# Sliding-window attention in a two-layer trunk: four heads per visit, score products alternating between the two 64-row halves of the array

## The chip, the cores and the metric

The kernel runs on one core of one Trainium2 chip. The time is the device time of one execution in microseconds (us), and the median of several runs stands for a kernel. A profile of one execution accompanies it. Engines are named as in the profile: PE is TensorE's matmul, PEld its weight load, DVE is VectorE, ACT is ScalarE, POOL is GpSimd, SP is SyncE.

## The reference

Two layers over 256 positions of width 1024. In each, one projection of the normed input feeds a gated linear recurrence and a sliding-window attention; both are merged, and a feed-forward block follows. What matters here is the attention: 16 query heads and 4 key/value heads of 64 columns, a window of 128, and one sink per query head that takes part in the softmax.

```python
def swa_with_sinks(q, k, v, sinks):
    ...
    s = jnp.einsum('bnqhgd,bnshd->bnhgqs', qb, kw).astype(jnp.float32) * (hd ** -0.5)
    ...
    mask = (delta >= 0) & (delta < WINDOW) & (kpos >= 0)
    s = jnp.where(mask[None, :, None, None], s, -jnp.inf)
    sink = sinks.astype(jnp.float32).reshape(1, 1, ATT_KV_HEADS, ATT_GROUP, 1, 1)
    m = jnp.maximum(jnp.max(s, axis=-1, keepdims=True), sink)
    p = jnp.exp(s - m)
    p = p / (jnp.sum(p, axis=-1, keepdims=True) + jnp.exp(sink - m))
    o = jnp.einsum('bnhgqs,bnshd->bnqhgd', p.astype(v.dtype), vw)
    return o.reshape(B, S, Hq * hd)
```

## The kernel before

The main stream is a sequence of projections. `proj` and `form_a` hold activations as the stationary operand and stream 512 columns of weight; `form_b` holds weights and streams 256 positions. Every f32 weight tile (`raw`, from memory) is split into two reduced-precision parts, `wh` by a cast on ACT and `wl` by a subtraction on DVE, and each product is three matmuls (`wh` with the activation's high part, `wl` with it, `wh` with its low part). Five buffers of each (`NW`) let the split run ahead of TensorE: `used()` gives a unit back and asks for the next.

All else runs beside the main stream as side work: Python generators (`keys`, `attention`, `recurrence`, the norms), which `run` advances at each `yield` of the main stream. A number that a side yields is how many main steps it sits out. A main step is six matmuls of 512 columns in the v and gate projections and twelve of 256 in the pb projection. The order in which instructions stand on each engine is then made by the tile scheduler out of this program order and its dependencies. [...]

The sixteen query heads lie in two tiles `qT[g]`, transposed, so that a head's 64 columns lie in rows 0 to 63 or 64 to 127: the row half `u` belongs to one key/value head, and `kT` holds its keys in the same half. Attention goes by pairs of heads, `kt` = 0 to 7 (`KT` = 8), two heads of one half in a visit. Round `kt` does `attend(kt)`, sits out `YA` = 2 main steps, does `turn(kt - 1)`, sits out `YB` = 2, does `values(kt - 1)`, sits out `YC` = 2:

- `attend` makes the scores. For query block t = 0 (128 keys) and t = 1 (256 keys) it issues two matmuls (tile `qk`), each with 64 contraction rows. DVE adds the mask and takes the row maximum into `stat` (the instruction is `CUSTOM_DVE_ANT_0` in the profile and `ISA` in the order), ACT takes the exponentials with their sum, DVE normalizes into `s` (tile `sp`).
- `turn` transposes the probabilities on TensorE (tile `pt`, six per visit), and ACT copies them to a second half of `sp`, `pT`.
- `values` multiplies with the values (tile `pv`): two heads, each into its own 64 output rows, that is, its own column half of the array. The result is split into `att` for the next projection.

Every PSUM tile has one 512-column bank. Tag `at` has two banks, `hg` two, and `mm` (the main stream) four. All tiles of the attention use `at` before. `spread` makes a row of scale factors by two matmuls (tile `rp`) out of two diagonal tiles `dg` that DVE writes; in the first attention rounds it stands between the v projections. The recurrence starts after the attention has ended, and shares the tag `sp` and the banks of `hg`.

Of the kernel before, what the change touches and what calls it, by code (L numbers as in the profile page):

```python
# [7 lines left out]
F32 = mybir.dt.float32  # L8
# [3 lines left out]
AF = mybir.ActivationFunctionType  # L12
ALU = mybir.AluOpType
AX = mybir.AxisListType

P = 128
D = 1024
S = 256
NT = S // P
DEPTH = 2  # L20
KT = D // P
HEADS = 8
QH = 16
KVH = 4
HD = 64
# [2 lines left out]
EPS = 1e-6  # L28
MIN_F = 1e-30
NRAW, NW = 3, 5  # L30
YA, YB, YC, YS, YO, YP, YD, YE, YQ = 2, 2, 2, 2, 2, 2, 3, 2, 5
NEG = -1e30

C_HQ, C_HF, C_HI, C_HG, C_AQ, C_AK, C_GA, C_GB = 0, 1024, 2048, 3072, 4096, 5120, 5632, 6656
# [6 lines left out]
def trunk(ctx, tc, x, norm1, w_in, lb_logits, hg_norm, attn_sinks, w_pa, w_pb, w_o, norm2,  # L41
# [18 lines left out]
    V, A, G, T = (Ordered(e) for e in (nc.vector, nc.scalar, nc.gpsimd, nc.tensor))  # L60
# [10 lines left out]
    sm = ctx.enter_context(tc.tile_pool(name="sm", bufs=2))  # L71
    pp = ctx.enter_context(tc.tile_pool(name="pp", bufs=2, space=bass.MemoryType.PSUM))

    def psum(name, tag="mm"):
        return pp.tile([P, 512], F32, tag=tag, name=name, bufs=4 if tag == "mm" else 2)

    def btile(shape, name, tag="b", dt=F32):
        return big.tile(shape, dt, tag=tag, name=name, bufs=6)

    def ztile(shape, name, tag="z", dt=F32):  # L80
        return sm.tile(shape, dt, tag=tag, name=name, bufs={"z": 4, "hx": 4, "rp": 2}[tag])
# [9 lines left out]
    ident = cp.tile([P, P], F32, tag="ident", name="ident")  # L91
# [17 lines left out]
    amask = cf[:, C_MASK:C_MASK + 256]  # L109
    nsink = cp.tile([P, DEPTH * QH], F32, tag="nsink", name="nsink")  # L110
# [148 lines left out]
    def split(hi, lo, src):  # L259
        A.copy(hi, src)  # L260
        V.tensor_tensor(lo, src, hi.bitcast(F32), ALU.subtract)
# [66 lines left out]
    def halves(name, tags="rr"):  # L328
        return [tuple(btile([P, 4, S], f"{name}{n}{g}", tags[g], F32R) for n in "hl") for g in range(2)]
# [29 lines left out]
    def layer(l, n1):  # L359
# [19 lines left out]
        def rope(buf, nh, t):  # L379
            v3 = buf.rearrange("p (h d) -> p h d", d=HD)  # L380
            co = cf[:, C_COS + 16 * t:C_COS + 16 * t + 16].rearrange("p (o c) -> p o c", o=1)
            si = cf[:, C_SIN + 16 * t:C_SIN + 16 * t + 16].rearrange("p (o c) -> p o c", o=1)
            ta = ztile([P, QH, 16], f"ropa{l}{t}{nh}", "rp")
            tb = ztile([P, QH, 16], f"ropb{l}{t}{nh}", "rp")
            V.tensor_tensor(ta[:, :nh], v3[:, :nh, 0:16], co.to_broadcast([P, nh, 16]), ALU.mult)
            V.tensor_tensor(tb[:, :nh, 0:8], v3[:, :nh, 8:16], si[:, :, 0:8].to_broadcast([P, nh, 8]), ALU.mult)
            V.tensor_tensor(tb[:, :nh, 8:16], v3[:, :nh, 0:8], si[:, :, 8:16].to_broadcast([P, nh, 8]), ALU.mult)
            V.tensor_tensor(v3[:, :nh, 0:16], ta[:, :nh], tb[:, :nh], ALU.add)

        akv = [ztile([P, 512], f"akv{l}{t}", "hx") for t in range(NT)]  # L390
        kT = ztile([P, 2, S], f"kT{l}", "hx")
        aq = [btile([P, D], f"aq{l}{t}") for t in range(NT)]
        qT = [btile([P, 4, S], f"qT{l}{g}") for g in range(2)]
# [3 lines left out]
        att = halves(f"att{l}")  # L397
# [3 lines left out]
        state = {}  # L401
# [11 lines left out]
        def queries(g):  # L413
            for t in range(NT):
                ps = psum(f"qp{l}{t}{g}", "at")
                for i in range(4):
                    T.transpose(ps[:, i * P:(i + 1) * P], aq[t][:, g * 512 + i * P:g * 512 + (i + 1) * P], ident)
                A.copy(qT[g][:, :, t * P:(t + 1) * P], ps.rearrange("p (i c) -> p i c", i=4))

        def attend(kt):  # L420
            g, u, i0 = kt // 4, (kt // 2) % 2, 2 * (kt % 2)
            pr = slice(u * 64, u * 64 + 64)
            hs = l * QH + 2 * kt
            s = state["sp"][:, kt % 2, 0]
            m = sm.tile([P, 4, 2, 2], F32, tag="stat", name=f"stat{l}{kt}", bufs=3)
            for t in range(NT):
                W = (t + 1) * P
                ps = psum(f"qk{l}{kt}{t}", "at")
                for i in range(2):
                    T.matmul(ps[:, i * W:(i + 1) * W], qT[g][pr, i0 + i, t * P:(t + 1) * P], kT[pr, g, 0:W],  # L430
                             start=True, stop=True)
                for i in range(2):
                    V.tensor_tensor_reduce(s[:, i, t * P:t * P + W], ps[:, i * W:(i + 1) * W], amask[:, 256 - W:256],
                                           op0=ALU.add, op1=ALU.max, scale=1.0, scalar=-3.0e38,
                                           accum_out=m[:, 0, t, i:i + 1])
            nsk = nsink[:, hs:hs + 2].rearrange("p (o h) -> p o h", o=1).to_broadcast([P, 2, 2])
            V.scalar_tensor_tensor(m[:, 1], m[:, 0], -0.125, nsk, ALU.mult, ALU.min)
            V.tensor_tensor(m[:, 2], m[:, 1], nsk, ALU.subtract)
            for t in range(NT):
                for i in range(2):  # L440
                    sv = s[:, i, t * P:t * P + (t + 1) * P]
                    A.activation(sv, sv, AF.Exp, bias=m[:, 1, t, i:i + 1], scale=0.125,
                                 accum_out=m[:, 0, t, i:i + 1])
            state["exp"] = A.activation(m[:, 2], m[:, 2], AF.Exp).ins
            V.tensor_tensor(m[:, 3], m[:, 0], m[:, 2], ALU.add)
            V.reciprocal(m[:, 3], m[:, 3])
            for t in range(NT):
                for i in range(2):
                    sv = s[:, i, t * P:t * P + (t + 1) * P]
                    V.tensor_scalar(sv, sv, m[:, 3, t, i:i + 1], None, ALU.mult)  # L450
            return s

        def turn(kt, s):
            pT = state["sp"][:, kt % 2, 1]
            ps = psum(f"pt0{l}{kt}", "at")
            for i in range(2):
                for t in range(NT):
                    T.transpose(ps[:, i * S + t * P:i * S + t * P + P], s[:, i, t * P:t * P + P], ident)
            A.copy(pT[:, :, 0:S], ps.rearrange("p (i c) -> p i c", i=2))
            ps = psum(f"pt1{l}{kt}", "at")  # L460
            for i in range(2):
                T.transpose(ps[:, i * P:(i + 1) * P], s[:, i, 2 * P:3 * P], ident)
            A.copy(pT[:, :, S:3 * P], ps[:, :S].rearrange("p (i c) -> p i c", i=2))
            return pT

        def values(kt, pT):
            g, kv = kt // 4, kt // 2
            po = psum(f"pv{l}{kt}", "at")
            vs = slice(256 + kv * HD, 256 + (kv + 1) * HD)
            for i in range(2):  # L470
                o = po[i * 64:i * 64 + 64, 0:S]
                T.matmul(o, akv[0][:, vs], pT[:, i, 0:S], start=True, stop=False)
                T.matmul(o[:, P:S], akv[1][:, vs], pT[:, i, S:3 * P], start=False, stop=True)
            split(att[g][0][:, kt % 4, :], att[g][1][:, kt % 4, :], po[:, :S])

        def attention():
            state["sp"] = sm.tile([P, 2, 2, 2, 384], F32, tag="sp", name=f"sp{l}", bufs=1)
            for t in range(NT):
                rope(aq[t], QH, t)
            yield YQ  # L480
            queries(0)
            yield 2
            prev = None
            for kt in range(KT + 1):
                cur = attend(kt) if kt < KT else None
                yield YA
                if prev is not None:
                    pT = turn(kt - 1, prev)
                    yield YB
                    values(kt - 1, pT)  # L490
                if kt == 1:
                    queries(1)
                prev = cur
                yield YC

        def decays(g):
# [203 lines left out]
        if l == 0:  # L700
            tables()
        finish(ksd)
        atd = start(attention(), 1)
        for c in range(2):
            if c == 1:
                spread()
            yield from proj(f"v{c}", lambda t, ps: evac_scaled(v[t][:, c * 512:(c + 1) * 512], ps, rs[t]))
        for g in range(2):
            for dst in fqk[g][:2]:
                for b in range(2):  # L710
                    ps = psum(f"pb{l}{g}{b}").rearrange("p (a c) -> p a c", a=2)
# [221 lines left out]
    for l in range(DEPTH):  # L933
        hold = []

        def whole():
            hold.append((yield from layer(l, nx)))

        run(whole())
        nx = hold[0]  # L940
# [53 lines left out]
```

## Time and profile before

| | before |
|---|---|
| median of 3 runs (lowest to highest) | 973.53 us (973.47 to 973.94) |
| the profiled execution, its own time | 973.66 us |
| its span, first to last instruction | 971.8 us |
| mean granted TensorE clock | 0.997 |
| instructions | 16199 |
| matmul records on PE | 6666 |
| attention, layer 0, first to last score product | starts at 57.8 us |
| attention, layer 1, last score product | 616.7 us |

In the profile an f32 matmul is two records on PE and two weight loads on PEld. A row of the timeline gives the start, the length, the engine, the line (all are line 55, a helper that issues everything), the operation, out<-in, the shape and how many records were merged; in brackets is idle time ahead and what ended it. Main matmuls overlap, so that the step from start to start is what one costs, not its length.

### The profile page before, as it was taken

The page shows a single profiled execution, that of the slowest core. Times are in us where ns is not written, and L with a number is a line of the kernel's source. Part 1 is how long each engine was busy: PE and PEld are TensorE (multiplying, and loading weights), DVE is VectorE, ACT ScalarE, POOL GpSimd, SP SyncE. Part 2 cuts the span into 40 slices and gives each one's busy share as a digit, 9 for nine tenths or more (in the row PEclk, how much of TensorE's full clock was granted, in tenths as well). Part 3 has the DMA queues.
Part 4 walks back from the last instruction along what each step waited for, and adds up shares of the span by engine and source line. Part 5 has one row for each costly group of instructions (what it writes and reads, how often), then busy time and mean ns, then how long its engine had stood idle before and what let it go on. Part 6 is the DMA issues. An engine that isn't in the chain of part 4 may idle for free.

```text
span 971.8 us, 16199 instructions
## 1 busy us (share of the span) xinstructions
PE 956.2 (98%) x6666; PEld 837.7 (86%) x6666; DVE 642.3 (66%) x1072; ACT 503.2 (52%) x810; POOL 17.8 (2%) x28
## 2 busy tenths in 40 slices
PE   7999999999999999999999999999999999999996
PEld 5879987788889999999878899887788899999995
DVE  6566667987587656555475666689857766556554
ACT  6556559555545444444365655775454544444442
POOL 1000000010000000000000000000000000000000
PEclk9999999999999999999999999999999999999998
DMA  8644444554445555655465444445545465555641
GB/s 281 228 153 131 131 131 131 174 172 133 171 150 185 188 177 192 195 175 189 157 209 182 130 131 133 130 132 173 172 152 174 153 195 193 197 173 182 203 136 44
DMA packets 110938, 161.24 MB, mean 166 GB/s; under 512 B 2769, under 2 KB 64401, under 8 KB 110865
## 3 DMA queue, kind: packets, MB, share of 16 engines
q1 hardware_dynamic: 110160, 159.12, 50.6%
q8 instruction: 52, 0.85, 0.3%
q10 hardware_dynamic: 704, 1.10, 0.3%
q14 instruction: 22, 0.17, 0.1%
HBM read 159.15 MB, written 1.05 MB: 165 GB/s over the span
## 4 chain that ended last, share of the span: by engine, by line
PE 91%; DVE 5%; ACT 2%; issue 1%; DMA 0%; POOL 0%; POOLq 0%; ACTq 0%; SPq 0%
PE pg L55 13%; PE pu L55 13%; PE acc L55 12%; PE pb L55 10%; PE ga L55 5%; PE v L55 5%; PE wo L55 5%; PE ya L55 5%; PE aq L55 4%; PE yb L55 3%; PE gate L55 3%; PE qk L55 3%; PE akv L55 2%; PE gb L55 2%; DVE wl L55 1%
## 5 line engine op out<-in xcount | busy, mean ns | idle before, releaser
L55 ACT CAST wh<-raw 128x1024 fp32r<-128x1024 f32 x300 | 314.4, 1049 | 358.9 <-PE pg L55 71.6
L55 DVE TENSOR_TENSOR wl<-raw,wh 128x1024 fp32r<-128x1024 f32 x300 | 366.5, 1223 | 199.3 <-ACT wh L55 198.0
L55 PE MATMUL pg<-xh_n,wh 128*128 128x256 f32 x352 | 99.8, 284 | 0.0
L55 PE MATMUL pu<-xh_n,wh 128*128 128x256 f32 x352 | 99.8, 283 | 0.0
L55 PE MATMUL pg<-xl_n,wh 128*128 128x256 f32 x352 | 99.7, 284 | 0.0
L55 PE MATMUL pu<-xh_n,wl 128*128 128x256 f32 x352 | 99.6, 283 | 0.0
L55 PE MATMUL pu<-xl_n,wh 128*128 128x256 f32 x352 | 99.6, 283 | 0.0
L55 PE MATMUL pg<-xh_n,wl 128*128 128x256 f32 x352 | 99.6, 283 | 0.0
L55 PE MATMUL pb<-xh_n,wh 128*128 128x256 f32 x256 | 75.4, 294 | 0.0
L55 PE MATMUL pb<-xl_n,wh 128*128 128x256 f32 x256 | 72.4, 283 | 0.0
L55 PE MATMUL pb<-xh_n,wl 128*128 128x256 f32 x256 | 72.4, 283 | 0.0
L55 PE MATMUL acc<-wl,ah 128*128 128x512 f32 x176 | 68.8, 391 | 0.0
L55 PE MATMUL acc<-wh,al 128*128 128x512 f32 x176 | 68.5, 389 | 0.0
L55 PE MATMUL acc<-wh,ah 128*128 128x512 f32 x176 | 68.3, 392 | 0.0
L55 PEld LDWEIGHTS pg<-xl_n,wh 128*128 128x128 f32 x352 | 67.5, 192 | 0.4
L55 PEld LDWEIGHTS pg<-xh_n,wh 128*128 128x128 f32 x352 | 67.5, 192 | 0.4
L55 PEld LDWEIGHTS pu<-xh_n,wh 128*128 128x128 f32 x352 | 67.6, 192 | 0.0
L55 PEld LDWEIGHTS pu<-xl_n,wh 128*128 128x128 f32 x352 | 67.6, 192 | 0.0
L55 PEld LDWEIGHTS pu<-xh_n,wl 128*128 128x128 f32 x352 | 67.6, 192 | 0.0
L55 PEld LDWEIGHTS pg<-xh_n,wl 128*128 128x128 f32 x352 | 67.5, 192 | 0.0
L55 PEld LDWEIGHTS pb<-xh_n,wh 128*128 128x128 f32 x256 | 48.9, 191 | 5.0 <-issue 5.0
L55 PEld LDWEIGHTS pb<-xl_n,wh 128*128 128x128 f32 x256 | 48.9, 191 | 0.0
(232 smaller groups left out, 1886.3 us busy)
## 6 DMA issues: line engine op xcount, KB each, us to landing
raw<-in_w_in SPq DMA_DIRECT2D x58, 1024.0 KB, 5.1
raw<-in_w_gate SPq DMA_DIRECT2D x22, 1024.0 KB, 5.2
raw<-in_w_up SPq DMA_DIRECT2D x22, 1024.0 KB, 5.2
raw<-in_w_down SPq DMA_DIRECT2D x22, 1024.0 KB, 5.0
raw<-in_w_pb SPq DMA_DIRECT2D x8, 1024.0 KB, 5.0
raw<-in_w_pa SPq DMA_DIRECT2D x8, 1024.0 KB, 5.1
raw<-in_w_o SPq DMA_DIRECT2D x8, 1024.0 KB, 5.0
raw<-in_w_in SPq DMA_DIRECT2D x4, 512.0 KB, 7.0
```

The source lines that it names most:

```text
L55: ins = call(*args, **kw)
```

## The change

Attention goes in four groups `n` of four heads, two heads in each row half, instead of eight pairs. `attend(n)` issues eight score matmuls; within a query block they alternate between the halves `u` = 0 and 1, which write to different PSUM banks. Block t = 0 uses the two `at` banks, t = 1 the two `hg` banks. The vector work per visit is twice as much (eight reduces, eight exponentials, eight normalizations), the statistics are computed per query block, and the number of heads in all is unchanged. `turn(n)` makes twelve transposes into three banks and copies back over `s` itself (three copies for four heads instead of four). `values(n)` does the products of four heads in one visit, for one key/value head after the other, with two banks. The main steps between become `YA`, `YB`, `YC` = 4, 3, 4; five rounds take the place of nine.

```diff
-YA, YB, YC, YS, YO, YP, YD, YE, YQ = 2, 2, 2, 2, 2, 2, 3, 2, 5
+YA, YB, YC, YS, YO, YP, YD, YE, YQ = 4, 3, 4, 2, 2, 2, 3, 2, 5
...
-        def attend(kt):
-            g, u, i0 = kt // 4, (kt // 2) % 2, 2 * (kt % 2)
-            pr = slice(u * 64, u * 64 + 64)
-            s = state["sp"][:, kt % 2, 0]
+        def attend(n):
+            g, i0 = n // 2, 2 * (n % 2)
+            s = state["sp"][:, n % 2]
...
-                ps = psum(f"qk{l}{kt}{t}", "at")
+                pss = [psum(f"qk{l}{n}{t}{u}", "hg" if t else "at") for u in range(2)]
                 for i in range(2):
-                    T.matmul(ps[:, i * W:(i + 1) * W], qT[g][pr, i0 + i, t * P:(t + 1) * P], kT[pr, g, 0:W],
-                             start=True, stop=True)
+                    for u in range(2):
+                        pr = slice(u * 64, u * 64 + 64)
+                        T.matmul(pss[u][:, i * W:(i + 1) * W], qT[g][pr, i0 + i, t * P:(t + 1) * P], kT[pr, g, 0:W],
+                                 start=True, stop=True)
...
-        def turn(kt, s):
-            pT = state["sp"][:, kt % 2, 1]
-            ps = psum(f"pt0{l}{kt}", "at")
-            for i in range(2):
+        def turn(n):
+            s = state["sp"][:, n % 2]
+            for u in range(2):
+                ps = psum(f"pt{l}{n}{u}", "at")
                 for i in range(2):
...
+                A.copy(s[:, 2 * u:2 * u + 2, 0:S], ps.rearrange("p (i c) -> p i c", i=2))
+            ps = psum(f"pt{l}{n}2", "hg")
+            for i in range(4):
                 T.transpose(ps[:, i * P:(i + 1) * P], s[:, i, 2 * P:3 * P], ident)
+            A.copy(s[:, :, S:3 * P], ps.rearrange("p (i c) -> p i c", i=4))
...
+        def values(n):
+            g, pT = n // 2, state["sp"][:, n % 2]
+            pos = [psum(f"pv{l}{n}{u}", "at") for u in range(2)]
+            for u in range(2):
+                vs = slice(256 + (2 * g + u) * HD, 256 + (2 * g + u + 1) * HD)
+                for i in range(2):
+                    o = pos[u][i * 64:i * 64 + 64, 0:S]
+                    T.matmul(o, akv[0][:, vs], pT[:, 2 * u + i, 0:S], start=True, stop=False)
+                    T.matmul(o[:, P:S], akv[1][:, vs], pT[:, 2 * u + i, S:3 * P], start=False, stop=True)
...
-            for kt in range(KT + 1):
-                cur = attend(kt) if kt < KT else None
+            for n in range(5):
+                if n < 4:
+                    attend(n)
                 yield YA
-                if prev is not None:
-                    pT = turn(kt - 1, prev)
+                if n:
+                    turn(n - 1)
                     yield YB
-                    values(kt - 1, pT)
-                if kt == 1:
+                    values(n - 1)
+                if n == 1:
                     queries(1)
```

Where the instructions stand now is shown at three places of layer 0. The first is PE at the first score products, between two matmuls of the v projection (`v_0` and `v_1` are its two PSUM tiles); before:

```order
L55 MATMUL v_1_480<-wl_454,xh_n_0_109 128x512
L55 MATMUL v_1_480<-wh_453,xl_n_0_110 128x512
L55 MATMUL qk_575<-kT_165,qT_168 128x128 x2
L55 MATMUL qk_580<-kT_165,qT_168 128x256 x2
L55 MATMUL v_0_608<-wh_506,xh_n_0_109 128x512
```

And now:

```order
L55 MATMUL v_1_480<-wh_453,xl_n_0_110 128x512
L55 MATMUL qk_575<-kT_165,qT_168 128x128
L55 MATMUL qk_576<-kT_165,qT_168 128x128
L55 MATMUL qk_575<-kT_165,qT_168 128x128
L55 MATMUL qk_576<-kT_165,qT_168 128x128
L55 MATMUL qk_585<-kT_165,qT_168 128x256
L55 MATMUL qk_586<-kT_165,qT_168 128x256
L55 MATMUL qk_585<-kT_165,qT_168 128x256
L55 MATMUL qk_586<-kT_165,qT_168 128x256
L55 MATMUL v_0_628<-wh_506,xh_n_0_109 128x512
```

Four matmuls in one half became eight that alternate between a tile of half 0 (575, 585) and one of half 1 (576, 586); in all other visits they stand the same way, but for the second of layer 1, where the halves change in blocks of one to three matmuls.

The second place is PE at the two `rp` matmuls of `spread`, a few main steps later; before, 26 main matmuls stand between the first score products and the first of them:

```order
L55 MATMUL v_0_608<-wl_541,xh_n_0_109 128x512
L55 MATMUL rp_n_0_600<-dg_n_00_601,ones 128x128
L55 MATMUL qk_645<-kT_165,qT_168 128x128 x2
L55 MATMUL v_0_608<-wh_540,xl_n_0_110 128x512
L55 MATMUL v_1_609<-wh_540,xh_n_0_109 128x512
L55 MATMUL rp_n_0_600<-dg_n_01_604,ones 128x128
L55 MATMUL v_1_609<-wl_541,xh_n_0_109 128x512
L55 MATMUL v_1_609<-wh_540,xl_n_0_110 128x512
L55 MATMUL qk_650<-kT_165,qT_168 128x256 x2
```

And now, behind 37 main matmuls (in layer 1 behind 43):

```order
L55 MATMUL v_0_628<-wh_570,xh_n_0_109 128x512
L55 MATMUL rp_n_0_620<-dg_n_00_621,ones 128x128
L55 MATMUL v_0_628<-wl_571,xh_n_0_109 128x512
L55 MATMUL v_0_628<-wh_570,xl_n_0_110 128x512
L55 MATMUL v_1_629<-wh_570,xh_n_0_109 128x512
L55 MATMUL v_1_629<-wl_571,xh_n_0_109 128x512
L55 MATMUL v_1_629<-wh_570,xl_n_0_110 128x512
L55 MATMUL rp_n_0_620<-dg_n_01_624,ones 128x128
```

The second visit, which the `rp` matmuls cut in two before, now follows them whole.

The third place is DVE from the reduces of the first visit to the diagonal tiles `dg` that `rp` reads; before:

```order
L55 ISA sp_487,stat_574<-qk_580,cf 128x256
L55 ISA stat_574 128x1
L55 TENSOR_TENSOR wl_623<-raw_522,wh_622 128x1024
L55 SCALAR_TENSOR_TENSOR stat_574<-stat_574,nsink 128x4
L55 TENSOR_TENSOR stat_574<-stat_574,nsink 128x4
L55 TENSOR_TENSOR stat_574<-stat_574 128x4
L55 RECIPROCAL stat_574<-stat_574 128x4
L55 TENSOR_SCALAR sp_487<-sp_487,stat_574 128x128 x2
L55 TENSOR_SCALAR sp_487<-sp_487,stat_574 128x256 x2
L55 TENSOR_SCALAR dg_n_00_601<-ident,r_n_00_113 128x128
L55 TENSOR_TENSOR wl_641<-raw_522,wh_640 128x1024
L55 TENSOR_SCALAR dg_n_01_604<-ident,r_n_01_114 128x128
```

And now, where the four 128-column reduces stand ahead of a `wl` and the four 256-column ones behind it:

```order
L55 ISA sp_487,stat_574<-qk_586,cf 128x256
L55 ISA stat_574 128x1
L55 SCALAR_TENSOR_TENSOR stat_574<-stat_574,nsink 128x4 x2
L55 TENSOR_TENSOR stat_574<-stat_574,nsink 128x4 x2
L55 TENSOR_TENSOR stat_574<-stat_574 128x8
L55 RECIPROCAL stat_574<-stat_574 128x8
L55 TENSOR_SCALAR sp_487<-sp_487,stat_574 128x128 x4
L55 TENSOR_SCALAR sp_487<-sp_487,stat_574 128x256 x4
L55 TENSOR_SCALAR dg_n_00_621<-ident,r_n_00_113 128x128
L55 TENSOR_TENSOR wl_661<-raw_522,wh_660 128x1024
L55 TENSOR_SCALAR dg_n_01_624<-ident,r_n_01_114 128x128
```

The diagonal tiles and the next `wl` moved behind twice the vector work of a visit.

More of the change, by code (lines that the diff above doesn't have):

```diff
@@ L418, in queries @@
                 A.copy(qT[g][:, :, t * P:(t + 1) * P], ps.rearrange("p (i c) -> p i c", i=4))
-        def attend(kt):
-            g, u, i0 = kt // 4, (kt // 2) % 2, 2 * (kt % 2)
-            pr = slice(u * 64, u * 64 + 64)
-            hs = l * QH + 2 * kt
-            s = state["sp"][:, kt % 2, 0]
-            m = sm.tile([P, 4, 2, 2], F32, tag="stat", name=f"stat{l}{kt}", bufs=3)
+        def attend(n):
+            g, i0 = n // 2, 2 * (n % 2)
+            s = state["sp"][:, n % 2]
+            m = sm.tile([P, 4, 2, 2, 2], F32, tag="stat", name=f"stat{l}{n}", bufs=3)
@@ L432, in attend @@
                 for i in range(2):
[L433 to L437, printed above, removed]
@@ L438, in attend @@
-            V.tensor_tensor(m[:, 2], m[:, 1], nsk, ALU.subtract)
-            for t in range(NT):
-                for i in range(2):
-                    sv = s[:, i, t * P:t * P + (t + 1) * P]
-                    A.activation(sv, sv, AF.Exp, bias=m[:, 1, t, i:i + 1], scale=0.125,
-                                 accum_out=m[:, 0, t, i:i + 1])
+                    for u in range(2):
+                        V.tensor_tensor_reduce(s[:, 2 * u + i, t * P:t * P + W], pss[u][:, i * W:(i + 1) * W],
+                                               amask[:, 256 - W:256], op0=ALU.add, op1=ALU.max, scale=1.0,
+                                               scalar=-3.0e38, accum_out=m[:, 0, t, u, i:i + 1])
@@ new lines, in attend @@
+            nsk = nsink.rearrange("p (l g u h) -> p l g u h", l=DEPTH, g=2, u=2)[:, l, g, :, i0:i0 + 2]
+            for t in range(NT):
+                V.scalar_tensor_tensor(m[:, 1, t], m[:, 0, t], -0.125, nsk, ALU.mult, ALU.min)
+                V.tensor_tensor(m[:, 2, t], m[:, 1, t], nsk, ALU.subtract)
+            for t in range(NT):
+                for u in range(2):
+                    for i in range(2):
+                        sv = s[:, 2 * u + i, t * P:t * P + (t + 1) * P]
+                        A.activation(sv, sv, AF.Exp, bias=m[:, 1, t, u, i:i + 1], scale=0.125,
+                                     accum_out=m[:, 0, t, u, i:i + 1])
@@ L447, in attend @@
             for t in range(NT):
-                for i in range(2):
-                    sv = s[:, i, t * P:t * P + (t + 1) * P]
-                    V.tensor_scalar(sv, sv, m[:, 3, t, i:i + 1], None, ALU.mult)
-            return s
-        def turn(kt, s):
-            pT = state["sp"][:, kt % 2, 1]
-            ps = psum(f"pt0{l}{kt}", "at")
[L456 to L461, printed above, removed]
-                T.transpose(ps[:, i * P:(i + 1) * P], s[:, i, 2 * P:3 * P], ident)
-            A.copy(pT[:, :, S:3 * P], ps[:, :S].rearrange("p (i c) -> p i c", i=2))
-            return pT
@@ L466, in values @@
[L466 to L474, printed above, removed]
+                for u in range(2):
+                    for i in range(2):
+                        sv = s[:, 2 * u + i, t * P:t * P + (t + 1) * P]
+                        V.tensor_scalar(sv, sv, m[:, 3, t, u, i:i + 1], None, ALU.mult)
@@ new lines, in turn @@
+        def turn(n):
+            s = state["sp"][:, n % 2]
+            for u in range(2):
+                ps = psum(f"pt{l}{n}{u}", "at")
+                for i in range(2):
+                    for t in range(NT):
+                        T.transpose(ps[:, i * S + t * P:i * S + t * P + P], s[:, 2 * u + i, t * P:t * P + P], ident)
+                A.copy(s[:, 2 * u:2 * u + 2, 0:S], ps.rearrange("p (i c) -> p i c", i=2))
+            ps = psum(f"pt{l}{n}2", "hg")
+            for i in range(4):
+                T.transpose(ps[:, i * P:(i + 1) * P], s[:, i, 2 * P:3 * P], ident)
+            A.copy(s[:, :, S:3 * P], ps.rearrange("p (i c) -> p i c", i=4))
@@ new lines, in values @@
+        def values(n):
+            g, pT = n // 2, state["sp"][:, n % 2]
+            pos = [psum(f"pv{l}{n}{u}", "at") for u in range(2)]
+            for u in range(2):
+                vs = slice(256 + (2 * g + u) * HD, 256 + (2 * g + u + 1) * HD)
+                for i in range(2):
+                    o = pos[u][i * 64:i * 64 + 64, 0:S]
+                    T.matmul(o, akv[0][:, vs], pT[:, 2 * u + i, 0:S], start=True, stop=False)
+                    T.matmul(o[:, P:S], akv[1][:, vs], pT[:, 2 * u + i, S:3 * P], start=False, stop=True)
+            for u in range(2):
+                kk = 2 * u + n % 2
+                split(att[g][0][:, kk, :], att[g][1][:, kk, :], pos[u][:, :S])
@@ L476, in attention @@
         def attention():
-            state["sp"] = sm.tile([P, 2, 2, 2, 384], F32, tag="sp", name=f"sp{l}", bufs=1)
+            state["sp"] = sm.tile([P, 2, 4, 384], F32, tag="sp", name=f"sp{l}", bufs=1)
             for t in range(NT):
@@ L482, in attention @@
             yield 2
-            prev = None
-            for kt in range(KT + 1):
-                cur = attend(kt) if kt < KT else None
+            for n in range(5):
+                if n < 4:
+                    attend(n)
                 yield YA
-                if prev is not None:
-                    pT = turn(kt - 1, prev)
+                if n:
+                    turn(n - 1)
                     yield YB
-                    values(kt - 1, pT)
-                if kt == 1:
+                    values(n - 1)
+                if n == 1:
                     queries(1)
-                prev = cur
                 yield YC
```

## The prediction

> **What bounds the kernel now.** I read the page's engine shares first, then the chain that ended last, then the waits.
>
> ```profile
> PE 956.2 (98%) x6666; PEld 837.7 (86%) x6666; DVE 642.3 (66%) x1072; ACT 503.2 (52%) x810; POOL 17.8 (2%) x28
> PEclk9999999999999999999999999999999999999998
> PE 91%; DVE 5%; ACT 2%; issue 1%; DMA 0%; POOL 0%; POOLq 0%; ACTq 0%; SPq 0%
> ACT wh L55 <- PE pg L55: 71.6, 44, 2.3
> ```
>
> TensorE is busy 98% of the span at a full granted clock and carries 91% of the chain. The casts that prepare weights wait for TensorE (ACT waits for PE to give a weight buffer back), not the other way round. So whatever takes time on TensorE comes off the end, one for one, as long as nothing new makes TensorE wait. All the rest is an account of TensorE time. I price a visit (a run of small matmuls between two matmuls of the main projection) by the start of the second main matmul behind it minus the start of the last one ahead of it, minus two ordinary steps.
>
> **A visit of score products (qk).** From the timeline of PE and the view of the tile qk:
>
> ```profile
> 57.25 0.39 PE L55 MATMUL v<-wl,xh_n 128*128 128x512 f32 x1
> 57.48 0.39 PE L55 MATMUL v<-wh,xl_n 128*128 128x512 f32 x1
> 57.80 1.57 PE L55 MATMUL qk<-kT,qT 64*128 64x128 f32 x8
> ...
> 59.64 0.40 PE L55 MATMUL v<-wl,xh_n 128*128 128x512 f32 x1
> ...
> 615.53 1.50 PE qk L55 x8
> L55 PE MATMUL qk<-kT,qT x128: 272/374/480, 57.8 to 616.7; 64*128 64x128 f32 x64, 64*128 64x256 f32 x64
> ```
>
> The main step is 57.48 - 57.25 = 0.23. The visit costs 59.64 - 57.48 - 0.46 = 1.70. It holds eight passes (each f32 matmul is two), four with 128 and four with 256 columns, all in one 64-row half. The 128 passes of the trace are 16 visits of eight, one for each of 8 head pairs in 2 layers; the piece of the chain at 615.53 is the last visit's. How much of 1.70 is streaming and how much is entering and leaving the 64-row form? One visit of layer 0 was cut in two by the scheduler, with rp matmuls around it:
>
> ```profile
> 65.10 0.39 PE L55 MATMUL v<-wl,xh_n 128*128 128x512 f32 x1
> 65.33 0.38 PE L55 MATMUL rp_n<-dg_n,ones 128*128 128x128 f32 x2
> 65.64 0.71 PE L55 MATMUL qk<-kT,qT 64*128 64x128 f32 x4
> ...
> 66.61 0.40 PE L55 MATMUL v<-wh,xh_n 128*128 128x512 f32 x1
> 66.84 0.38 PE L55 MATMUL rp_n<-dg_n,ones 128*128 128x128 f32 x2
> ...
> 67.30 0.40 PE L55 MATMUL v<-wh,xl_n 128*128 128x512 f32 x1
> 67.62 1.13 PE L55 MATMUL qk<-kT,qT 64*128 64x256 f32 x4
> ...
> 69.02 0.39 PE L55 MATMUL v<-wl,xh_n 128*128 128x512 f32 x1
> ```
>
> 66.61 - 65.10 - 0.46 = 1.05 for rp and the 128 part; 67.30 - 66.61 - 0.46 = 0.23 for an rp alone; 69.02 - 67.30 - 0.46 = 1.26 for the 256 part. So the cut visit costs 1.05 - 0.23 + 1.26 = 2.08 where a whole one costs 1.70. The same eight passes with one more entry and exit: a switch costs 0.38, streaming 1.32. Before, qk takes 14 x 1.70 + 2 x 2.08 = 28.0 us (the second visit of layer 1 is cut in the same way, and I take the same price).
>
> **Do two halves run side by side?** No row of before mixes the two row halves in one visit, so this is the unknown. The nearest row is the product with the values (pv), which writes two column halves:
>
> ```profile
> 86.23 0.28 PE L55 MATMUL pb<-xl_n,wh 128*128 128x256 f32 x1
> 86.35 0.28 PE L55 MATMUL pb<-xh_n,wl 128*128 128x256 f32 x1
> 86.56 0.88 PE L55 MATMUL pv<-sp,akv 128*64 128x256 f32 x8
> ...
> 87.59 0.28 PE L55 MATMUL pb<-xl_n,wh 128*128 128x256 f32 x1
> L55 PE MATMUL pv<-sp,akv x128: 272/326/431, 73.7 to 633.9; 128*64 128x256 f32 x64, 128*64 128x128 f32 x64
> 73.70 0.20 PEld L55 LDWEIGHTS pv<-sp,akv 128*64 128x64 f32 x4 [0.35 <-ACT wh L55]
> 78.46 0.41 PEld L55 LDWEIGHTS qk<-kT,qT 64*128 64x128 f32 x3
> ```
>
> A pv visit has the same eight passes, four of 256 and four of 128 columns, and costs 87.59 - 86.35 - 0.24 = 1.00. With the same switch of 0.38 that is 0.62 of streaming, 0.47 of the 1.32 in a qk visit. Two column halves therefore run side by side here, and their weight loads too: four loads lie within 0.20, while three qk loads in one half take 0.41, 0.11 apart. Ends for the new qk visit, which has sixteen passes: side by side 1.32 + 0.38 = 1.70 (the pv row), one after the other 2.64 + 0.38 = 3.02 (the qk row). I take 1.70: the two halves have their own rows of the array and, in the new code, their own PSUM banks, so they are apart in the same sense as the two column halves are.
>
> **The sum, part by part.**
> - qk: 16 visits become 8. At 1.70 each 13.6 instead of 28.0: -14.4 (at 3.02 each: -3.8).
> - pv: 16 visits of 1.00 become 8 with twice the streaming and one switch, 1.24 + 0.38 = 1.62: 13.0 instead of 16.0, -3.0. Ends: 0, if the switch stood inside the streaming, and -3.0.
> - Transposes (pt): equal in number, 12 per visit instead of 6. Their rows show no switch to save:
>
> ```profile
> 82.83 0.28 PE L55 MATMUL pb<-xh_n,wl 128*128 128x256 f32 x1
> 82.95 0.82 PE L55 MATMUL pt<-ident,sp 128*128 128x128 f32 x6
> ...
> 83.72 0.28 PE L55 MATMUL pb<-xl_n,wh 128*128 128x256 f32 x1
> ```
>
> 83.72 - 82.83 - 0.24 = 0.65 for six, 0.11 each, which is their streaming: 0. One copy from PSUM less per four heads falls on ACT, which is 52% busy: 0.
> - The in-place turned probabilities (s is overwritten) add a wait: the reduces of visit n+2 write where the pv matmuls of visit n read. In the order two visits lie between, so it is over: 0.
> - Twelve main steps per four heads (2 x 6) become 11, and five rounds of 11 replace nine of 6: the attention ends one step later (62 against 61), and the recurrence after it starts one step later, in the same visits: 0. The sigmoids that follow the last exp move ahead, under projections: 0.
> - The vector work of a visit doubles and lies in one stretch. Who waits for it? In layer 0 the rp matmul, behind a dg on DVE that stands behind the whole chain of the first visit:
>
> ```profile
> 58.54 0.29 DVE L55 CUSTOM_DVE_ANT_0 sp<-qk,cf 128x128 f32<-128x128 f32 x1 [1.90 <-PE qk L55]
> 58.76 0.29 DVE L55 CUSTOM_DVE_ANT_0 sp<-qk,cf 128x128 f32<-128x128 f32 x1
> 59.41 0.43 DVE L55 CUSTOM_DVE_ANT_0 sp<-qk,cf 128x256 f32<-128x256 f32 x1 [0.35 <-PE qk L55]
> 60.10 1.22 DVE L55 TENSOR_TENSOR wl<-raw,wh 128x1024 fp32r<-128x1024 f32 x1
> 61.24 0.15 DVE L55 SCALAR_TENSOR_TENSOR stat<-stat,nsink 128x4 f32<-128x4 f32 x1
> 61.43 0.40 ACT L55 ACTIVATE sp<-sp,stat 128x128 f32<-128x128 f32 x1 [1.91 <-DVE stat L55]
> 63.42 0.16 DVE L55 TENSOR_TENSOR stat<-stat 128x4 f32<-128x4 f32 x1 [1.83 <-ACT stat L55]
> 63.84 1.01 DVE L55 TENSOR_SCALAR sp<-sp,stat 128x128 f32<-128x128 f32 x4
> 64.76 0.28 DVE L55 TENSOR_SCALAR dg_n<-ident,r_n 128x128 f32<-128x128 f32 x1
> ```
>
> In the new order four reduces of 0.22 (58.54 to 58.76) start at 58.54, then wl (60.10 to 61.24: 1.14), four of 0.35 (59.41 to 60.10 is two), one step of statistics 0.19: the exps begin at 62.1. They took 61.43 to 63.42 = 1.99, with about 0.2 of it the last small one; twice as many take 3.8: 65.9. Then 0.42 and twice 0.92 (63.84 to 64.76): dg starts at 68.2 and is usable at 68.6. The rp stands behind 37 main matmuls instead of 26; the second of them starts at 59.64, so TensorE is there at 59.64 + 36 x 0.23 = 67.9. It waits 0.7 us. In layer 1 the rp stands behind 43, 1.4 us more, and does not wait: +0.7 in all (ends: 0 and 2). The weights themselves have more room: the next wl is written by 70, and TensorE needs it after a unit of 24 pb matmuls that follows the second visit, some 6 us later.
>
> [...]
>
> Sum: -14.4 - 3.0 + 0.7 = -16.7. The profiled execution took 973.66 with a span of 971.8; the median of the runs is 973.53, 0.1 away. 973.53 - 16.7 = **956.8 us**.
>
> **Rivals.**
> 1. The halves overlap only in part (960.1). For it: no row shows loads into two row halves. If the sixteen loads still come 0.11 apart, they bound the visit: 16 x 0.11 + 0.38 = 2.14, eight of them 17.1, so -10.9 - 3.0 + 0.5 = -13.4. Against it: the pv loads lie together. [...]
> 2. The change does not do what it says: the halves run one after the other. Then qk gives -3.8 and pv -3.0, rp comes late enough for its dg: 966.7. Against it: pv.
> 3. Slower: a change of the row half costs like a change of form. A visit then has seven changes, eight visits 56. The switch of 0.38 is an entry and an exit, 0.19 each; 56 x 0.19 = 10.6 on top of serial visits gives -6.8 + 10.6 = +3.8: 977.3. It decides against the change from 6.8 / 56 = 0.12 us per change. For it: entering a form does cost. Against it: in pv the column half changes within the visit and 0.62 leaves no room for it.
>
> **Chances.** Side by side 0.72 (956.8; its own range is 954.8 to 960: streams that shrink to 0.47 as in pv, 8 x (1.24 + 0.38) = 13.0, and no wait give 973.53 - 15.0 - 3.0 = 955.5, less the spread of the runs; no saving at pv gives 959.8). Rival 1 0.10, rival 2 0.08, rival 3 0.10, in which a price near 0.12 leaves 0.03 within no change. The range 954.8 to 963.0 holds the first two cases, 0.82, less a little for waits I did not see. 0.2% is 1.9 us, about what this kernel's runs can tell from no change; faster by more: 0.72 + 0.10 + 0.08 = 0.90; the same 0.03; slower 0.07.
>
> **What would show it.** In the trace after: eight qk visits of sixteen passes, each with a cost near 1.70 (2.1: rival 1; 3.0: rival 2; above 3.0: rival 3); pv visits near 1.62; DVE busy unchanged, with about 0.7 us of TensorE idle ahead of the first rp of layer 0 and none in layer 1; the span near 955.1. A new wait of PE for wl or wh within the attention would make the forecast too low; so would a wait of the qp matmuls for the PSUM banks that both pv now hold.

## The result, and the profile after

The changed kernel takes 957.56 us (957.36 to 957.66) against 973.68 us for the kernel before on the same chip (973.47 to 973.94): a ratio of 0.9834, 95% interval 0.9817 to 0.9851. The change is worth 16.1 us; 16.7 was forecast (956.8). The profiled execution has a span of 955.8, 16.0 less than before.

From the page of the changed kernel: busy time of the engines, granted TensorE clock by slices, the shares of the chain that ended last.

```profile
span 955.8 us, 16173 instructions
PE 940.6 (98%) x6666; PEld 830.2 (87%) x6666; DVE 639.3 (67%) x1056; ACT 502.6 (53%) x794; POOL 16.4 (2%) x28
PEclk9999999999999999999999999999999999999999
PE 96%; ACT 1%; DMA 1%; DVE 1%; issue 0%; POOL 0%; POOLq 0%; ACTq 0%
```

The number of matmul records is the same (6666), the mean granted clock is 0.998 (0.997 before), and TensorE is still busy 98% of the span. Its busy time fell by 15.6 (956.2 to 940.6), so nearly all of the gain is TensorE time; little of it is idle time of TensorE that went away.

The timeline of PE at the first score visit of the changed kernel (start, length, shape, records merged):

```profile
57.30 0.39 PE L55 MATMUL v<-wh,xl_n 128*128 128x512 f32 x1
57.62 1.58 PE L55 MATMUL qk<-kT,qT 64*128 64x128 f32 x16
59.13 0.50 PE L55 MATMUL v<-wh,xh_n 128*128 128x512 f32 x1
59.46 0.40 PE L55 MATMUL v<-wl,xh_n 128*128 128x512 f32 x1
```

59.46 - 57.30 - 0.46 = 1.70: sixteen passes cost what eight cost before. Seven of the eight score visits cost 1.70 or 1.71. The eighth is the second of layer 1. The timeline of PE there:

```profile
539.50 0.39 PE L55 MATMUL v<-wh,xl_n 128*128 128x512 f32 x1
539.73 0.38 PE L55 MATMUL rp_n<-dg_n,ones 128*128 128x128 f32 x2
540.04 2.46 PE L55 MATMUL qk<-kT,qT 64*128 64x128 f32 x16
...
542.65 0.28 PE L55 MATMUL pb<-xl_n,wh 128*128 128x256 f32 x1
```

The groups of PE by shape from 540.0 to 540.9, then the timeline of ACT:

```profile
L55 PE MATMUL qk<-kT,qT 64*128 64x128 f32 x4 | 0.7, 297 | 0.0
L55 PE MATMUL qk<-kT,qT 64*128 64x256 f32 x2 | 0.6, 378 | 0.0
```

```profile
539.23 1.38 ACT L55 ACTIVATE v<-v,r_n 128x512 f32<-128x512 f32 x2 [1.17 <-PE v L55]
540.51 0.36 ACT L55 COPY rb_n<-rp_n 128x256 f32<-128x256 f32 x1
```

The two steps around it are 0.23 and 0.12, so rp and qk cost 542.65 - 539.50 - 0.35 = 2.80 together, and 2.58 without the 0.22 of an rp. The rp tile holds one of the two `at` banks until ACT has copied it, and ACT gets to that at 540.51, behind the scaling of v. The 128-column products of half 1 need that bank, and it is free at 540.87 (540.51 + 0.36). Until 540.9 only six of the sixteen passes have started, all of half 0. The other ten are the products that need the bank and those that stand behind them in the order of this visit.

The timeline of PE at the first rp of layer 0, the row of PE's waits that belongs to it, and the first dg on DVE's timeline:

```profile
67.42 0.39 PE L55 MATMUL v<-wh,xh_n 128*128 128x512 f32 x1
68.46 0.49 PE L55 MATMUL rp_n<-dg_n,ones 128*128 128x128 f32 x2 [0.65 <-DVE dg_n L55]
...
69.02 0.40 PE L55 MATMUL v<-wh,xl_n 128*128 128x512 f32 x1
```

```profile
PE rp_n L55 <- DVE dg_n L55: 0.7, 1, 0.7
```

```profile
68.12 0.28 DVE L55 TENSOR_SCALAR dg_n<-ident,r_n 128x128 f32<-128x128 f32 x1
```

The rp waits 0.65 for its diagonal tile and costs 69.02 - 67.42 - 0.46 = 1.14 instead of 0.23. Layer 1 has no such wait. Last, the timeline of PE at the first visit with the values:

```profile
84.53 0.28 PE L55 MATMUL pb<-xh_n,wl 128*128 128x256 f32 x1
84.74 1.57 PE L55 MATMUL pv<-sp,akv 128*64 128x256 f32 x16
...
86.46 0.28 PE L55 MATMUL pb<-xl_n,wh 128*128 128x256 f32 x1
```

86.46 - 84.53 - 0.24 = 1.69, the same for all eight.

### The profile page after: what moved, and what is told of

It reads as the page before. It is cut to its first block, busy times and chain, and to the rows that moved or that the text cites. A ratio compares the mean times of both kernels' runs of the same rounds, so it can differ in the third digit from the quotient of the medians.

```text
span 955.8 us, 16173 instructions
## 1 busy us (share of the span) xinstructions
PE 940.6 (98%) x6666; PEld 830.2 (87%) x6666; DVE 639.3 (67%) x1056; ACT 502.6 (53%) x794; POOL 16.4 (2%) x28
## 3 DMA queue, kind: packets, MB, share of 16 engines
HBM read 159.15 MB, written 1.05 MB: 168 GB/s over the span
## 4 chain that ended last, share of the span: by engine, by line
PE 96%; ACT 1%; DMA 1%; DVE 1%; issue 0%; POOL 0%; POOLq 0%; ACTq 0%
PE pg L55 13%; PE pu L55 13%; PE acc L55 12%; PE pb L55 10%; PE yb L55 5%; PE ga L55 5%; PE gb L55 5%; PE gate L55 5%; PE ya L55 5%; PE wo L55 5%; PE aq L55 5%; PE v L55 4%; PE akv L55 2%; PE qk L55 1%; PE pv L55 1%; PE o L55 1%
```

## The experiments

The theory: the two row halves stream side by side, a visit pays its switch once, and every microsecond of TensorE comes off the end. The rivals: the gain comes from the longer visits alone; it depends on the strict alternation of the halves; what is saved at the rp matmuls comes back elsewhere. All kernels but the two repeats of the changed kernel have `spread` one projection earlier, called the early spread here, so that neither wait of the rp matmuls disturbs the score visits.

**The early spread itself.**

```diff
-            if c == 1:
+            if c == 0:
                 spread()
```

> One edit: spread (the dg tiles on DVE and the rp matmuls) is called ahead of the first v projection instead of ahead of the second. Theory: the wait of rp for dg in layer 0 goes (rp cost 1.14 there, 0.23 elsewhere: 0.9 us), and the second visit of layer 1, whose order was broken because a bank was still held by rp, becomes a whole one (2.58 there against 1.70: 0.9 us): 957.56 - 1.8 = 955.8. Rival (these are hidden, or the dg and rp wait elsewhere): no change, 957.6.

Measured: 957.46 us (956.89 to 957.79), ratio 0.9829 [0.9815, 0.9844], no change against the changed kernel. All eight score visits cost 1.70 now, 13.6 together, and no wait for dg is left in PE's list of waits. But the rp matmuls did not get cheap. The timeline of PE in layer 0:

```profile
52.52 0.39 PE L55 MATMUL v<-wl,xh_n 128*128 128x512 f32 x1
52.93 0.49 PE L55 MATMUL rp_n<-dg_n,ones 128*128 128x128 f32 x2
...
53.48 0.40 PE L55 MATMUL v<-wh,xh_n 128*128 128x512 f32 x1
```

This rp costs 53.48 - 52.52 - 0.46 = 0.50, since its dg stands behind a wl on DVE (the wl takes 1.22 from 51.38, the dg starts at 52.59, the rp at 52.93), and the second one 0.48, where 0.23 is what an rp costs without a wait. A visit of the query transposes (qp) then waits for the bank of a pv tile and costs 0.77 instead of 0.44. In the trace layer 0 gives about 0.1 and layer 1 about 0.7; of the 1.8 that the two waits are worth, 0.8 shows. The profiled execution also reached its 120th projection matmul 1.1 later than that of the changed kernel, all of it in the first 40 us, and that hid the rest. The early spread is not the reason of the late start: the two kernels with cut visits below have it too and reach that matmul only 0.2 and 0.3 later, the two repeats of the changed kernel 0.4 to 0.5 later. The kernels that follow were forecast from 955.8; what counts is their distance from the 957.46 measured here.

**One half for all.** Do two halves run side by side? This kernel leaves the second half of the rows out: its heads get scores from the first half's queries and keys.

```diff
-                        pr = slice(u * 64, u * 64 + 64)
+                        pr = slice(0, 64)
```

> All score products use row half 0 (the products of the second half are made from the first half's queries and keys, so those heads hold other scores); spread is called one projection earlier, as in e4_early_spread, so that rp is out of the way. Counts, shapes, banks and order are those of e4. Theory (the gain is the overlap of the two row halves): nothing can overlap, a qk visit of sixteen passes costs 2 x 1.32 + 0.38 = 3.02 instead of 1.70, eight of them 10.6 us more than e4: about 966.4. Rival (the gain is in fewer, longer visits and their place): visits stay near 1.70 and the time near e4's 955.8.

Measured: 967.52 us, ratio 0.9932 [0.9915, 0.9948], 10.1 above the early spread. The timeline of PE at the first score visit:

```profile
59.26 0.39 PE L55 MATMUL v<-wh,xl_n 128*128 128x512 f32 x1
59.58 2.88 PE L55 MATMUL qk<-kT,qT 64*128 64x128 f32 x16
...
62.74 0.40 PE L55 MATMUL v<-wl,xh_n 128*128 128x512 f32 x1
```

The same sixteen passes in the same order, all in one half, cost 62.74 - 59.26 - 0.46 = 3.02, the serial end of the forecast (3.02) to the last digit. Eight visits take 24.1 instead of 13.6, 10.5 more; the time is 10.1 more, and the qp visit no longer costs its extra 0.33 here. The banks, the counts and the order are the same, so the overlap of the halves is shown, and it alone is worth 10 us.

**Blocks of two and of four matmuls.** Must the halves alternate matmul by matmul? In the first kernel a half does two matmuls (four passes) before the other does two:

```diff
-                for i in range(2):
-                    for u in range(2):
+                for u in range(2):
+                    for i in range(2):
                         pr = slice(u * 64, u * 64 + 64)
```

> On top of e4: within a query block both matmuls of half 0 come first, then both of half 1 (blocks of four passes instead of two). Theory (each half is fed as a stream of its own, as the column halves of pv are, where blocks of four passes overlap fully): a visit stays at 1.70, the time at e4's 955.8. Rival (strict order, only neighbours across a change of half overlap): three changes per visit instead of seven, the visit near 2.5, eight of them 6 to 7 us more: about 962.

In the second all four matmuls (eight passes) of one half stand before those of the other, and the order is pinned:

```diff
+            every = [[psum(f"qk{l}{n}{t}{u}", "hg" if t else "at") for u in range(2)] for t in range(NT)]
+            for u in range(2):
+                for t in range(NT):
...
+                    for i in range(2):
...
+                        T.matmul(every[t][u][:, i * W:(i + 1) * W], qT[g][pr, i0 + i, t * P:(t + 1) * P],
+                                 kT[pr, g, 0:W], start=True, stop=True)
...
```

> On top of e4: all four matmuls of half 0 first (both query blocks, eight passes), then the four of half 1. Theory (two streams without a limit on how far ahead one may run): 1.70 per visit, 955.8. Rival, a limited look ahead, for which the broken visit of layer 1 speaks, where half 1 began only behind six passes of half 0: the visit lies between 1.70 and 3.02, and if nothing overlaps, at 3.02 and 966.4. I lean to the rival, near 2.6 and 963.

Measured: blocks of two 957.64 us, ratio 0.9832 [0.9817, 0.9847]; blocks of four 961.40, ratio 0.9870 [0.9856, 0.9885], which is 3.9 above the early spread. The timelines of PE at the first visit, first of blocks of two, then of blocks of four:

```profile
59.00 0.39 PE L55 MATMUL v<-wh,xl_n 128*128 128x512 f32 x1
59.32 1.68 PE L55 MATMUL qk<-kT,qT 64*128 64x128 f32 x16
...
61.27 0.39 PE L55 MATMUL v<-wl,xh_n 128*128 128x512 f32 x1
```

```profile
59.17 0.39 PE L55 MATMUL v<-wh,xl_n 128*128 128x512 f32 x1
59.49 2.13 PE L55 MATMUL qk<-kT,qT 64*128 64x128 f32 x16
...
61.89 0.39 PE L55 MATMUL v<-wl,xh_n 128*128 128x512 f32 x1
```

61.27 - 59.00 - 0.46 = 1.81 and 61.89 - 59.17 - 0.46 = 2.26, between 1.70 and 3.02. Where does the second half begin in the last case? Its groups of PE by shape, first in 59.48 to 60.03 and then in 60.31 to 60.47 (a group holds what runs in that stretch):

```profile
L55 PE MATMUL qk<-kT,qT 64*128 64x128 f32 x4 | 0.7, 297 | 0.0
...
L55 PE MATMUL qk<-kT,qT 64*128 64x128 f32 x3 | 0.6, 306 | 0.0
L55 PE MATMUL qk<-kT,qT 64*128 64x256 f32 x2 | 0.6, 377 | 0.0
```

and the changed kernel in the first 0.55 us of its visit:

```profile
L55 PE MATMUL qk<-kT,qT 64*128 64x128 f32 x8 | 0.7, 298 | 0.0
```

In 0.55 us the changed kernel starts eight 128-column passes, four of each half; blocks of four start only four, those of the first half. In the later stretch these have ended (they started before 60.03; the first takes 0.37, the others 0.27), and yet three 128-column passes run beside two of 256 columns. The three are of the second half, while two of the first half's four 256-column passes, which stand ahead of them in the program, have not started. The visit is 2.26 - 1.70 = 0.56 longer, which is the time of the four passes that ran alone. A bank that comes free late is not the reason: the second visit, at 72.66, has the same 2.13 from its first pass to its end as the one above, and the early spread uses the same banks at the same places and has visits of 1.70. So the change of half need not stand at every matmul: four passes of one half ahead of the other cost 0.11 a visit, eight cost 0.56; what sets these two costs no run shows. The rival of a strict order (2.5 a visit in blocks of two) falls with the 1.81, and the theory of two streams without a limit (1.70 in blocks of four) with the 2.26, which lies in the range of its rival (1.70 to 3.02) and below the 2.6 that I leaned to. The theory of 1.70 in blocks of two misses by the 0.11, which the time does not tell from the early spread (957.64 against 957.46).

**Visits cut in two.** Is the length of a visit worth anything? One kernel puts a main step of projection between the two query blocks of a score visit, the other between the two key/value heads of a visit with the values; the step is taken from the pause that follows.

```diff
+                if t:
+                    yield 1
                 W = (t + 1) * P
```

> The kernel with the early spread, and each score visit cut in two by one main step of projection between its 128-column part and its 256-column part; nothing else moves. Theory (a visit pays 0.38 once for leaving and entering the full form, and the rest is streaming): eight more switches, 8 x 0.38 = +3.0 on 957.5: 960.5, each of the sixteen half visits 0.38 plus 0.44 or 0.88. Rival (the gain is the overlap of the two halves alone, a longer visit brings nothing): 957.5.

```diff
             for u in range(2):
+                if u:
+                    yield 1
                 vs = slice(256 + (2 * g + u) * HD, 256 + (2 * g + u + 1) * HD)
```

> The kernel with the early spread, and each visit of products with the values cut in two between its two key/value heads, as in the kernel before; nothing else moves. Theory (switch of 0.38 once per visit): half visits of 1.00 as before, 2 x 1.00 - 1.69 = 0.31 more for each of eight, +2.5 to +3.0 on 957.5: 960.0 to 960.5. Rival (the switch lies inside the streaming): 957.5.

Measured: 960.12 us, ratio 0.9858 [0.9844, 0.9872], and 959.67, ratio 0.9853 [0.9839, 0.9867]: 2.7 and 2.2 above the early spread. The timeline of PE with the score visits cut, then with the value visits cut (one half visit of the second group):

```profile
58.53 0.39 PE L55 MATMUL v<-wh,xl_n 128*128 128x512 f32 x1
58.85 0.72 PE L55 MATMUL qk<-kT,qT 64*128 64x128 f32 x8
...
59.84 0.39 PE L55 MATMUL v<-wl,xh_n 128*128 128x512 f32 x1
...
60.76 0.40 PE L55 MATMUL v<-wh,xl_n 128*128 128x512 f32 x1
61.09 1.13 PE L55 MATMUL qk<-kT,qT 64*128 64x256 f32 x8
...
62.49 0.40 PE L55 MATMUL v<-wl,xh_n 128*128 128x512 f32 x1
```

```profile
106.24 0.28 PE L55 MATMUL pb<-xh_n,wl 128*128 128x256 f32 x1
106.45 0.88 PE L55 MATMUL pv<-sp,akv 128*64 128x256 f32 x8
...
107.48 0.28 PE L55 MATMUL pb<-xl_n,wh 128*128 128x256 f32 x1
```

The halves of a score visit cost 59.84 - 58.53 - 0.46 = 0.85 and 62.49 - 60.76 - 0.46 = 1.27, together 0.41 more than the 1.71 of the whole one. A half visit with the values costs 107.48 - 106.24 - 0.24 = 1.00, twice that is 0.31 more than 1.69. The times are a little under eight times these (3.3 and 2.5), in the first kernel because the qp visit got its 0.33 back. So a switch costs 0.4 at the scores and 0.3 at the values, and the length of the visits is worth its part.

**Both rp waits taken away.** The dg tiles get two buffers and are written before the aq projection; the rp matmuls stand ahead of the first v projection. The changed kernel ran beside it unchanged.

```diff
+        def diag(self):
+            self.dg = [sm.tile([P, P], F32, tag="dg", name=f"dg_{self.name}{t}", bufs=2) for t in range(NT)]
+            for t in range(NT):
+                tc.keep_in_program_order(V.tensor_scalar(self.dg[t], ident, self.r[t], None, ALU.mult))
...
         ksd = start(keys(), 1)
+        n1.diag()
...
-            if c == 1:
+            if c == 0:
                 spread()
```

> The changed kernel as it is, timed beside the three that follow. Every theory: 957.6, and again a first rp of layer 0 that waits about 0.65 for its dg, and a second score visit of layer 1 that costs about 2.6 where the others cost 1.70.

> Takes both waits away that the rp matmuls brought to the changed kernel: both dg tiles have buffers of their own and are written before the aq projection, and the rp matmuls stand ahead of the first v projection in both layers. Theory (TensorE time alone counts, and the waits were worth their TensorE time): in layer 0 the two rp cost 0.3 instead of 1.37, one qp visit may still cost 0.33 more for its bank; in layer 1 the rp cost 0.3 instead of 0.45 and the second score visit 1.70 instead of 2.58. Together -1.07 + 0.33 - 0.15 - 0.88 = -1.8: 955.8. Rival (as in the kernel with the early spread, the time comes back elsewhere, whatever is done with rp): 957.5, no change.

Measured: 957.48 us (957.25 to 957.68), ratio 0.9831 [0.9817, 0.9845]; the changed kernel beside it 957.84 (957.62 to 958.00), ratio 0.9833 [0.9820, 0.9847]. By the time alone the rival holds. The repeat of the changed kernel shows both losses again: a wait of 0.6 for dg, and 2.80 for the rp and the second score visit of layer 1. The trace says where: PE's waits and its timeline in layer 0's second norm:

```profile
PE rp_n L55 <- DVE dg_n L55: 0.6, 2, 0.3
```

```profile
294.47 0.45 PE L55 MATMUL rp_n<-dg_n,ones 128*128 128x128 f32 x2
295.19 0.49 PE L55 MATMUL rp_n<-dg_n,ones 128*128 128x128 f32 x2 [0.27 <-DVE dg_n L55]
```

In the two attentions together this kernel gains 1.6 on the changed kernel beside it. But the second norm uses `spread` too, and there the two rp matmuls now come one behind the other instead of some 3.8 us apart, each behind its dg: 1.05 and 1.11 for the two norms, where 0.5 was paid. My edit brought 1.1 back; the next kernel leaves the second norm as it was.

```diff
             for t in range(NT):
-                dg = sm.tile([P, P], F32, tag="dg", name=f"dg_{self.name}{t}", bufs=1)
-                tc.keep_in_program_order(V.tensor_scalar(dg, ident, self.r[t], None, ALU.mult))
+                if self.dg is None:
+                    dg = sm.tile([P, P], F32, tag="dg2", name=f"dg_{self.name}{t}", bufs=1)
+                    tc.keep_in_program_order(V.tensor_scalar(dg, ident, self.r[t], None, ALU.mult))
+                else:
+                    dg = self.dg[t]
                 T.matmul(rp[:, t * P:(t + 1) * P], ones, dg, start=True, stop=True)
...
```

> As the kernel with the early diagonal, but the second norm of each layer keeps one buffer and the order that it has in the changed kernel, with its two rp matmuls apart. Theory: that norm's rp cost 1.05 and 1.11 in the kernel with the early diagonal, 0.49 a layer with the matmuls apart, so 1.2 comes back and the 1.6 gained in the two attentions stays: 957.5 - 1.2 = 956.3, and 1.5 under the changed kernel run beside it. Rival (what is saved there returns elsewhere whatever is done): no change against the changed kernel, within 0.4.

> The changed kernel as it is, beside the other. Every theory: 957.6 to 957.9.

Measured: 956.28 us (956.02 to 956.46), ratio 0.9819 [0.9805, 0.9832]; the changed kernel beside it 957.98 (957.78 to 958.15), ratio 0.9836 [0.9823, 0.9850]. The runs of the two do not touch, and the difference is 1.7. The timeline of PE in layer 0, where the four passes of both rp now stand in one visit without a wait:

```profile
46.03 0.63 PE L55 MATMUL rp_n<-dg_n,ones 128*128 128x128 f32 x4
```

So the two losses of the changed kernel were worth their TensorE time, and this is the fastest of the kernels.

## Why the prediction was right, point by point

The forecast of 956.8 rested on -14.4 (qk), -3.0 (pv), +0.7 (rp), and on zeros. By the same pricing of the visits in the trace after:

| term | forecast | measured |
|---|---|---|
| qk | -14.4 | 7 x 1.70 + 2.58 = 14.5 instead of 28.0: -13.5 |
| pv | -3.0 | 8 x 1.69 = 13.5 instead of 16.0: -2.5 |
| first rp of layer 0 | +0.7 | 1.14 instead of 0.23: +0.9 |
| pt | 0 | 10.5 instead of 10.6: -0.1 |
| recurrence | 0 | -0.9 |
| sum | -16.7 | -16.1 |

- **qk.** Side by side was right, in all seven undisturbed visits, and the kernel with one half for all shows the cause. What the step missed is 0.9 in layer 1: there I looked only at whether rp waits for dg, and not at what waits behind rp. It holds an `at` bank, and the score products of the next visit need both. The order of that visit, in blocks of one to three matmuls, stands under The change and got no term. In it six passes of half 0 stand ahead of half 1; the early spread takes away the wait and this order together, so no run shows how much of the 0.9 is the order's. The forecast named a bank wait, but for the qp matmuls, which do not wait in the changed kernel (0.44 each).
- **pv.** The 1.62 took one switch of 0.38 out of two visits of 1.00. The cut kernel gives 0.31 for a switch at the values. I had carried the price from the score visits to the values, and 0.07 in eight visits is the 0.5 missing here.
- **rp.** The wait was forecast at 0.7 in layer 0 and none in layer 1, and it measured 0.65 and none, by the cause that was forecast: dg starts at 68.12, where 68.2 was forecast. Its visit costs 0.9 more: the rp starts 1.04 behind the last main matmul (68.46 - 67.42) instead of 0.23, and the next main matmul follows later as well (0.24 behind the rp instead of 0.14).
- **Recurrence.** I took it to be unchanged one step later. It gained: PE's list of waits before has two rows that the list after lacks:

```profile
PE lc L55 <- DVE p L55: 0.6, 2, 0.3
PE lv L55 <- DVE f L55: 0.4, 2, 0.2
```

These waits and what follows them go; the lb visits cost 0.7 more in return. No run separates the one later step from the moved vector work, so the reason of this 0.9 is open. It makes up for the 0.9 at the bank by luck: the sum misses by only 0.6 because a gain that was not forecast and a loss that was not forecast are of one size.

- **Rivals.** Partial overlap (2.14 a visit): no, 1.70. Serial (3.02, 966.7): no, but it is what the kernel with one half for all gives, 967.5. A change of half with a price (slower): no; the changed kernel changes the half at every matmul and costs 0.11 a visit less than blocks of two.
- **Two halves against one.** The streaming of a visit goes from 3.02 - 0.38 = 2.64 in one half to 1.70 - 0.38 = 1.32 in two, a factor of 2.0.

## What to carry to other kernels

Here products with 64 contraction rows cost about half when those of the two row halves stood at most two matmuls apart (a visit of sixteen passes 1.70 when alternating and 1.81 in blocks of two, against 3.02 in one half; each half had PSUM banks of its own; no run tried a shared one). A visit of such products should be as long as the vector work behind it allows, since each one paid 0.3 (values) to 0.4 us (scores) here. When a visit takes more banks, look for who else holds one at that time, not only for who waits for data: here both small losses sat at a two-matmul helper beside the visits. A helper that is called in two places should be changed for one of them first.

## What the runs showed of the hardware that was not expected

What a score visit costs when one row half is written ahead of the other. With the halves alternating matmul by matmul it costs 1.70; with four passes of one half written ahead of the other half's first (blocks of two matmuls) 1.81; with eight (blocks of four) 2.26; with all sixteen in one half 3.02. In the case of eight the other half started about 0.55 late, but, by the rows by shape of that kernel, ahead of passes that stand before it in the program: from 60.31 to 60.47 three of its 128-column passes ran beside two of the first half's four 256-column passes, and the other two had not started. No run shows what decides when a pass of the other half starts.
